# Summing the first mixer's conditioning vectors on VectorE instead of TensorE in the prologue of a two-layer block

## The chip, the cores and the metric

The kernel runs on one core of one Trainium2 chip. A core has TensorE (PE in the profile; its weight loads are shown as PEld), VectorE (DVE), ScalarE (ACT), GpSimd (POOL) and SyncE (SP), which issues most of the DMAs. Each engine works through its own instruction stream in order, and engines wait for one another by semaphores. The metric is the device time of one execution in microseconds, as the median of several runs. The profile is one separate execution.

## The reference, cut to what matters

A block of two layers works on 512 tokens of 1024 channels, in fp32. Each layer has a mixer (a gated linear recurrence in layer 0, dilated attention in layer 1) and a feed-forward part. Six conditioning vectors per layer scale, shift and gate what goes in and out:

```python
cond = jax.nn.silu(c)                                     # c is 1 x 1024
mod = (cond @ ada_w[layer] + ada_b[layer])[:, None, :]    # ada_w[layer] is 1024 x 6144
sh1, sc1, g1, sh2, sc2, g2 = jnp.split(mod, 6, axis=-1)
u = rms_norm(h, norm_g[layer, 0]) * (1.0 + sc1) + sh1
y = hgrn2_mixer(u, ...)                                   # begins with u @ w_in, 1024 x 4096
```

The change touches `sh1` and `sc1` of layer 0, that is, two matrix-vector products of a 1024 x 1024 block of `ada_w[0]` with `cond`, and the fp32 copy of `u` that they give.

## The kernel before

Products of fp32 accuracy are made of three TensorE passes over operands split in a rounded high part (`hi`, type fp32r) and the rest (`lo`): high by high, low by high, high by low. ScalarE makes the high part, and VectorE subtracts it from the fp32 original to make the low part.

The prologue (everything up to `pre.close()`) normalises and transposes the input to `xnT` (channels on the partitions, eight channel blocks of 128, 512 tokens each), finds `sh1` and `sc1`, makes `u` and its parts `uh` and `ul`, and computes the value projection `v_tok` of the first mixer. It goes through the eight channel blocks `e` in turn. For each block it needs

- `first[e]`, 1 MB: the columns of `ada_w[0]` that give `sh1` and `sc1` of this block, laid out as 8 row blocks `kt` of 128 rows on the partitions, each with 2 x 128 columns. Three buffers hold it; `load(e)` fetches it and the block's 128 rows of the value weights (512 KB).
- `group_steps(e)` (line 1523): eight TensorE matmuls of 256 columns in the code (16 in the profile, each with its weight load) that sum the eight row blocks, weighted with `cond`, into one PSUM bank with the partial sums spread over the partitions; ScalarE copies them to `facc` (line 1526).
- `sum_steps(e)` (line 1531): two TensorE matmuls of one column each (four in the profile), which sum `facc` over the partitions.
- `col_steps(e)` (lines 1536 and 1538): three VectorE instructions on 128x1, which add the bias and make the two columns of `cols`.
- `u_hi(e)` (line 1543): ScalarE makes `uh` of the block as `xnT * scale + shift`.
- `u_lo(e, ...)` (lines 1549 and 1550): VectorE makes the fp32 `u` in the same way, and then `ul = u - uh`.
- `w_hi(e)` and `w_lo(e)` (lines 1559 and 1562): ScalarE and VectorE split the value weights of the block.
- `v_pass(e, which, hf, t)` (line 1568): one TensorE pass of 512 columns. `which` 0 needs `uh` and the high weights, 1 needs `ul`, 2 needs the low weights. In the loop each `which` has seven passes, one for each tile in `tiles` (four token tiles by two column halves, less one); the eighth tile has no free PSUM bank and is made up at the end, in 18 passes after block 6 and 6 after block 7.

The prologue stands under `manual_schedule` for TensorE, VectorE, ScalarE and GpSimd, so these four run their instructions in the order in which the code is written. Only the order on SyncE's DMA queue is left to the compiler. In the loop over `e` from 1 to 7, the code for block `e` contains the conditioning of block `e + 1`: `group_steps(e + 1)` stands behind the `which` 0 passes, `sum_steps`, `col_steps`, `u_hi` and `u_lo` of block `e + 1` stand between the `which` 1 and the `which` 2 passes. Block 4's weights are split at the end of turn 2 and not at the start of turn 3, and turns 2 and 3 also hold a few small operations on the lower bounds (`lower_a` on ScalarE, `lower_b`, four VectorE instructions). After `u_hi(7)` the weights of the next stage are fetched by `st.fill()`, split in pieces (lines 135 and 136), and the main stage begins with TensorE matmuls on line 1856. The rest of the kernel, with an order by a planner whose costs are constants in the code, is not touched.

## Time and profile before

| what | value |
|---|---|
| median of 3 runs | 1436.22 us (1434.48 to 1436.47) |
| the profiled execution's own time | 1430.78 us |
| its span | 1429.0 us |
| TensorE busy | 1402.2 us, 98% of the span |
| VectorE busy | 1151.8 us, 81% |
| ScalarE busy | 823.5 us, 58% |
| start of the last value pass of the prologue | 73.05 us |
| start of the first matmul of the main stage | 73.27 us |

Times in a timeline are counted from the start of the span. A row of the timeline gives start, duration, engine, line, operation, what is written and read, and, in brackets, how long the engine sat idle before it and which instruction ended that. Successive instructions of one engine can overlap in these records, so what matters for a sequence is the distance from start to start. In a view by groups a row gives the number of instructions, their busy time in us and the mean of one in ns.

### The profile page before, as it was taken

The page shows a single profiled execution, that of the slowest core. Times are in us where ns is not written, and L with a number is a line of the kernel's source. Part 1 is how long each engine was busy: PE and PEld are TensorE (multiplying, and loading weights), DVE is VectorE, ACT ScalarE, POOL GpSimd, SP SyncE. Part 2 cuts the span into 40 slices and gives each one's busy share as a digit, 9 for nine tenths or more (in the row PEclk, how much of TensorE's full clock was granted, in tenths as well). Part 3 has the DMA queues.
Part 4 walks back from the last instruction along what each step waited for, and adds up shares of the span by engine and source line. Part 5 has one row for each costly group of instructions (what it writes and reads, how often), then busy time and mean ns, then how long its engine had stood idle before and what let it go on. Part 6 is the DMA issues. An engine that isn't in the chain of part 4 may idle for free. (4 is left out here: it accounts for less than half of the span.)

```text
span 1429.0 us, 25206 instructions
## 1 busy us (share of the span) xinstructions
PE 1402.2 (98%) x9785; PEld 1300.5 (91%) x9785; DVE 1151.8 (81%) x1838; ACT 823.5 (58%) x1539; POOL 208.5 (15%) x179
## 2 busy tenths in 40 slices
PE   8999999999999999999999999999999999999998
PEld 6788999899999988888989999999988899999887
DVE  4599889587888799778888977888776978888994
ACT  4443434465555643376648878477885555656651
POOL 1023112130111113140001010001012211110020
PEclk9999999999999999999999999999999999999999
DMA  9665655132344378423254452444362334334451
GB/s 309 180 207 191 206 178 177 60 110 73 114 119 119 118 248 290 138 95 122 93 152 126 111 154 66 122 138 130 99 200 87 104 104 119 111 104 163 155 177 59
DMA packets 213896, 201.09 MB, mean 141 GB/s; under 512 B 8920, under 2 KB 170640, under 8 KB 213520
## 3 DMA queue, kind: packets, MB, share of 16 engines
q1 hardware_dynamic: 210800, 192.71, 43.2%
q10 hardware_dynamic: 1952, 6.65, 1.3%
q8 instruction: 77, 1.26, 0.4%
q0 software_dynamic: 1024, 0.12, 0.2%
q14 instruction: 43, 0.35, 0.1%
HBM read 192.30 MB, written 5.30 MB: 138 GB/s over the span
## 5 line engine op out<-in xcount | busy, mean ns | idle before, releaser
L1856 PE MATMUL ps_mm<-apart,hiq 128*128 128x256 f32 (+1 forms) x608 | 137.4, 320 | 2.0 <-ACT xs L2348 1.2
L1856 PE MATMUL ps_mm<-uh,hiq 128*128 128x256 f32 (+1 forms) x416 | 134.5, 323 | 0.0
L1856 PE MATMUL ps_mm<-uh,loq 128*128 128x256 f32 (+1 forms) x416 | 131.1, 315 | 0.2 <-DVE loq L2281 0.2
L1856 PE MATMUL ps_mm<-ul,hiq 128*128 128x256 f32 (+1 forms) x416 | 131.0, 315 | 0.0
L1856 PEld LDWEIGHTS ps_mm<-apart,hiq 128*128 128x128 f32 x608 | 99.9, 191 | 8.3 <-ACT xs L2348 1.8
L967 DVE TENSOR_TENSOR loq<-raw,hiq 128x1024 fp32r<-128x1024 f32 x72 | 85.0, 1221 | 20.1 <-ACT hiq L963 20.1
L976 PE MATMUL ps_mm<-th,hiq 128*128 128x256 f32 x360 | 99.0, 275 | 0.0
L976 PE MATMUL ps_mm<-tl,hiq 128*128 128x256 f32 x360 | 99.0, 275 | 0.0
L976 PE MATMUL ps_mm<-th,loq 128*128 128x256 f32 x360 | 99.0, 275 | 0.0
L1856 PE MATMUL ps_mm<-apart,loq 128*128 128x256 f32 (+1 forms) x304 | 95.4, 314 | 0.6 <-DVE loq L2370 0.6
L947 POOL TENSOR_TENSOR raw<-raw 128x512 f32<-128x512 f32 x36 | 47.9, 1331 | 320.0 <-DVE spare L943 165.2
L963 ACT CAST hiq<-raw 128x1024 fp32r<-128x1024 f32 x72 | 72.3, 1049 | 21.2 <-DVE raw L951 16.6
L1856 PEld LDWEIGHTS ps_mm<-uh,loq 128*128 128x128 f32 x416 | 79.4, 191 | 4.7 <-DVE loq L2281 0.4
L1856 PEld LDWEIGHTS ps_mm<-uh,hiq 128*128 128x128 f32 x416 | 79.4, 191 | 4.4 <-issue 0.2
L1856 PEld LDWEIGHTS ps_mm<-ul,hiq 128*128 128x128 f32 x416 | 79.4, 191 | 4.1 <-issue 0.5
L976 PEld LDWEIGHTS ps_mm<-th,hiq 128*128 128x128 f32 x360 | 69.1, 192 | 0.1
L976 PEld LDWEIGHTS ps_mm<-tl,hiq 128*128 128x128 f32 x360 | 69.1, 192 | 0.0
L976 PEld LDWEIGHTS ps_mm<-th,loq 128*128 128x128 f32 x360 | 69.1, 192 | 0.0
L1856 PEld LDWEIGHTS ps_mm<-apart,loq 128*128 128x128 f32 x304 | 58.0, 191 | 3.9 <-DVE loq L2370 1.0
L596 PE MATMUL ps_mm<-ul,hi 128*128 128x256 f32 (+1 forms) x176 | 55.3, 314 | 1.6 <-DVE ul L695 1.6
L595 PE MATMUL ps_mm<-uh,hi 128*128 128x256 f32 (+1 forms) x176 | 55.4, 315 | 0.0
L597 PE MATMUL ps_mm<-uh,lo 128*128 128x256 f32 (+1 forms) x176 | 55.2, 314 | 0.0
(547 smaller groups left out, 4840.7 us busy)
## 6 DMA issues: line engine op xcount, KB each, us to landing
raw<-in_ffn_w_in_dram SPq DMA_DIRECT2D x144, 256.0 KB, 4.0
raw<-in_ada_w_dram SPq DMA_DIRECT2D x30, 1024.0 KB, 6.1
raw<-in_attn_w_in_dram SPq DMA_DIRECT2D x64, 256.0 KB, 4.2
raw<-in_ffn_w_out_dram SPq DMA_DIRECT2D x13, 1024.0 KB, 5.5
raw<-in_attn_w_in_dram SPq DMA_DIRECT2D x12, 1024.0 KB, 5.2
raw<-in_hgrn_w_in_dram SPq DMA_DIRECT2D x11, 1024.0 KB, 5.3
rawx<-in_ffn_w_out_dram SPq DMA_DIRECT2D x9, 1024.0 KB, 6.1
third<-in_ada_w_dram SPq DMA_DIRECT2D x8, 1024.0 KB, 7.0
```

Of the source, the lines that this page charges most:

```text
L595: pe.matmul(ps, ah, bh, start=start, stop=False, skip_group_check=part)
L596: pe.matmul(ps, ah, bl, start=False, stop=False, skip_group_check=part)
L597: pe.matmul(ps, al, bh, start=False, stop=stop, skip_group_check=part)
L947: pool.tensor_add(r[:, 2], r[:, 2], r[:, 0])
L963: act.copy(hi, src)
L967: dve.tensor_sub(lo, src, hi.bitcast(F32))
L976: pe.matmul(LAID(ps), w[x][:, a], TAKE(us[kt][y]), start=begin and kt + m == 0, stop=kt == 3 and m == 2, skip_group_check=True)
L1856: pe.matmul(LAID(dst()), x, TAKE(y), start=begin and i == 0, stop=i == len(todo) - 1, skip_group_check=True)
```

## The change

For the channel blocks 2 to 7 the sum over the row blocks is made by VectorE: `group_on_dve(e)` is one `tensor_scalar` and seven `scalar_tensor_tensor` on 128x256, each of which reads the result of the one before. `sum_steps` is as before and now sums this accumulator (`dacc`, two buffers) over the partitions. Blocks 0 and 1 keep `group_steps`. The sum of block `e + 2` is written into turn `e`, behind `u_lo(e + 1)`; `sum_steps`, `col_steps`, `u_hi` and `u_lo` of block `e + 1` move ahead of the `which` 1 passes. For blocks 2 to 7 the fp32 copy `u` is made by ScalarE, behind `u_hi`, and VectorE keeps the subtraction. The load of block 4 moves ahead of the loop, and in the loop `load(e + 4)` stands in place of `load(e + 3)`.

```diff
@@ -1525,6 +1525,14 @@
             accs_of[e] = fresh(sp, [P, 2, P], "facc", 1)
             act.copy(accs_of[e], ps.rearrange("p (v n) -> p v n", v=2))
 
+        def group_on_dve(e):
+
+            a = accs_of[e] = fresh(sp, [P, 2, P], "dacc", 2)
+            both = lambda t: t.rearrange("p v n -> p (v n)")
+            dve.tensor_scalar(both(a), both(first[e][:, 0]), cond[:, 0:1], None, op0=OP.mult)
+            for kt in range(1, KT):
+                dve.scalar_tensor_tensor(both(a), both(first[e][:, kt]), cond[:, kt:kt + 1], both(a), op0=OP.mult, op1=OP.add)
+
         def sum_steps(e):
 
             for v in (1, 0):
@@ -1546,7 +1554,10 @@
             if e not in us:
                 us[e] = fresh(sp, [P, S], "u", 2)
             u = us[e][:, tok]
-            dve.tensor_scalar(u, xnT[:, e, tok], cols[:, 1, e:e + 1], cols[:, 0, e:e + 1], op0=OP.mult, op1=OP.add)
+            if e > 1:
+                act.activation(u, xnT[:, e, tok], AF.Identity, bias=cols[:, 0, e:e + 1], scale=cols[:, 1, e:e + 1])
+            else:
+                dve.tensor_scalar(u, xnT[:, e, tok], cols[:, 1, e:e + 1], cols[:, 0, e:e + 1], op0=OP.mult, op1=OP.add)
             sub.tensor_sub(ul[:, e, tok], u, uh[:, e, tok].bitcast(F32))
 
         def w_tiles(q):
@@ -1673,21 +1684,24 @@
             col_steps(1)
             u_hi(1)
             u_lo(1, dve)
+            load(4)
+            group_on_dve(2)
             for e in range(1, KT):
                 if e + 1 < KT and e != 3:
                     w_hi(e + 1)
                     w_lo(e + 1, dve)
-                for which in (0, 1):
-                    for i in tiles:
-                        v_pass(e, which, *i)
-                    if which == 0 and e + 1 < KT:
-                        group_steps(e + 1)
+                for i in tiles:
+                    v_pass(e, 0, *i)
                 if e + 1 < KT:
                     sum_steps(e + 1)
-                    load(e + 3)
                     col_steps(e + 1)
                     u_hi(e + 1)
                     u_lo(e + 1, dve)
+                    load(e + 4)
+                if e + 2 < KT:
+                    group_on_dve(e + 2)
+                for i in tiles:
+                    v_pass(e, 1, *i)
                 if e == 2:
                     w_hi(4)
                     w_lo(4, dve)
```

## The prediction

> **What bounds the kernel now.** I read the page's head first, then the first 75 us, where all edits lie: a table of busy times in stretches, then the timeline of one turn of the loop, engine by engine.

> ```profile
> span 1429.0 us, 25206 instructions
> PE 1402.2 (98%) x9785; PEld 1300.5 (91%) x9785; DVE 1151.8 (81%) x1838; ACT 823.5 (58%) x1539; POOL 208.5 (15%) x179
> 50.00:60.00 10.00, 10.00 (x71) 7.07 (x69) 5.43 (x11) 3.87 (x5) 0.00 (x0) 1.00 0.20 69
> ```

> TensorE is idle for at most 27 us of the span, so the end of the prologue moves the end of the kernel nearly one to one. In the loop TensorE is full, VectorE 54%, ScalarE 39%, and GpSimd has nothing. The TensorE timeline of one turn, and of the last conditioning sum and what follows it:

> ```profile
> 42.82 0.50 PE L1531 MATMUL ps_b<-ones,facc 128*128 128x1 f32 x4
> 46.47 1.07 PE L1523 MATMUL ps_b<-first,cond_tiles 128*32 128x256 f32 x16
> 47.47 0.70 PE L1568 MATMUL ps_a<-hi,ul 128*128 128x512 f32 x2
> 49.08 0.50 PE L1531 MATMUL ps_b<-ones,facc 128*128 128x1 f32 x4
> ...
> 61.60 0.50 PE L1531 MATMUL ps_b<-ones,facc 128*128 128x1 f32 x4
> 61.96 0.68 PE L1568 MATMUL ps_a<-late,uh 128*128 128x512 f32 x2
> 63.55 0.38 PE L1568 MATMUL ps_b<-hi,uh 128*128 128x512 f32 x1
> 73.27 0.38 PE L1856 MATMUL ps_mm<-uh,hi 128*128 128x512 f32 x1
> ```

> A turn takes 49.08 - 42.82 = 6.26 us, of which the sum over row blocks takes 1.00. That is what the change takes off TensorE: about 5.3 us a turn would be left if nothing else waited. VectorE and ScalarE in such a turn:

> ```profile
> 30.91 0.16 DVE L1536 TENSOR_TENSOR cols<-ps_b,adab 128x1 f32<-128x1 f32 x1 [2.79 <-PE ps_b L1531]
> 31.11 0.16 DVE L1538 SCALAR_TENSOR_TENSOR cols<-cols,smallB 128x1 f32<-128x1 f32 x1
> 31.18 0.15 DVE L1536 TENSOR_TENSOR cols<-ps_b,adab 128x1 f32<-128x1 f32 x1
> 31.44 0.55 DVE L1549 TENSOR_SCALAR u<-xnT,cols 128x512 f32<-128x512 f32 x1
> 32.22 0.69 DVE L1550 TENSOR_TENSOR ul<-u,uh 128x512 fp32r<-128x512 f32 x1 [0.23 <-ACT uh L1543]
> ...
> 31.37 0.81 ACT L1543 ACTIVATE uh<-xnT,cols 128x512 fp32r<-128x512 f32 x1 [2.12 <-DVE cols L1536]
> 32.09 1.03 ACT L1559 CAST hi<-raw 128x1024 fp32r<-128x1024 f32 x1
> ```

> VectorE's longest wait of the turn, 2.79 us, is for TensorE's sum. The reader is to see that VectorE has room as a share, but in the written order that room lies ahead of the column step, while everything the change adds lies in one loop: sum on TensorE, columns, `uh`, `u`, `ul`, next group on VectorE, next sum.

> **The change, part by part.** Six groups (blocks 2 to 7) leave TensorE, and with them six ScalarE copies `facc`. VectorE gets six chains of one `tensor_scalar` and seven `scalar_tensor_tensor` on 128x256, each reading the last one's result. No such chain is in the trace; the nearest is the same sum with 512 columns, in the next stage:

> ```profile
> 78.66 0.75 DVE L1803 SCALAR_TENSOR_TENSOR shared<-raw,cond,shared 128x512 f32<-128x512 f32 x1
> 79.32 1.22 DVE L1906 TENSOR_TENSOR loq<-raw,hiq 128x1024 fp32r<-128x1024 f32 x1
> 80.46 0.74 DVE L1803 SCALAR_TENSOR_TENSOR shared<-raw,cond,shared 128x512 f32<-128x512 f32 x1
> 81.24 3.11 DVE L1803 SCALAR_TENSOR_TENSOR shared<-third,cond,shared 128x512 f32<-128x512 f32 x4
> ...
> 73.44 0.49 DVE L1801 TENSOR_SCALAR shared<-raw,cond 128x512 f32<-128x512 f32 x1 [0.57 <-DMA raw<-in_ada_w_dram]
> 73.96 0.75 DVE L1803 SCALAR_TENSOR_TENSOR shared<-raw,cond,shared 128x512 f32<-128x512 f32 x1
> ...
> 10.96 0.75 DVE L1501 TENSOR_SCALAR late<-h,rr 128x1024 f32<-128x1024 f32 x1 [0.67 <-POOL rr L1498]
> ...
> L1550 DVE TENSOR_TENSOR ul<-u,uh 128x512 fp32r<-128x512 f32 x7 | 4.8, 693 | 2.0 <-ACT uh L1543 2.0
> L1550 DVE TENSOR_TENSOR ul<-u,uh 128x256 fp32r<-128x256 f32 x1 | 0.4, 425 | 0.1
> L1803 DVE SCALAR_TENSOR_TENSOR shared<-raw,cond,shared 128x512 f32<-128x512 f32 x10 | 8.2, 822 | 0.0
> ```

> Four in a chain take 3.11 us; with 0.75 for the last, the start-to-start distance is (3.11 - 0.75) / 3 = 0.787. An independent successor starts after 79.32 - 78.66 = 0.66. Going from 512 to 256 columns saves 0.693 - 0.425 = 0.268 on a two-input operation (the pair on line 1550): so 0.52 from link to link and 0.39 from the last link to whatever follows. The first operation, from 0.75 at 1024 and 0.49 at 512, comes to about 0.36, and with the 0.03 that 73.44, 0.49 and 73.96 leave, to 0.39. The chain holds VectorE for **g = 0.39 + 6 x 0.52 + 0.39 = 3.9 us** (an estimate from these rows). Below, if links did not wait for one another: 0.39 + 7 x 0.39 = 3.1. Above, by the mean 0.82 of line 1803 in place of 0.75: 3.9 + 7 x 0.07 = 4.4. I take 3.9, since the chain of four has the same form and operands.

> *The copy `u`* moves from VectorE (0.55) to ScalarE. It stands behind `uh`, which another ScalarE operation follows after 32.09 - 31.37 = 0.72, and lasts 0.81 like `uh`. The subtraction now waits for it, where it waited for `uh`: 0.72 later. In the written order nothing can use VectorE in that time, because the next group stands behind the subtraction. So this edit costs 0.72 a block on the loop.

> [...]

> What else is in the loop: from VectorE's subtraction to its successor, the four small operations of `lower_b`, the first subtraction of the loop, and the way of a finished sum through TensorE:

> ```profile
> 44.74 0.69 DVE L1550 TENSOR_TENSOR ul<-u,uh 128x512 fp32r<-128x512 f32 x1 [0.30 <-ACT uh L1543]
> 45.35 0.20 DVE L1578 RECIPROCAL lbt<-lbt 128x8 f32<-128x8 f32 x1
> 46.06 1.22 DVE L1562 TENSOR_TENSOR lo<-raw,hi 128x1024 fp32r<-128x1024 f32 x1
> ...
> 25.96 0.69 DVE L1550 TENSOR_TENSOR ul<-u,uh 128x512 fp32r<-128x512 f32 x1 [0.30 <-ACT uh L1543]
> ...
> 23.44 0.37 ACT L1526 COPY facc<-ps_b 128x256 f32<-128x256 f32 x1 [2.62 <-PE ps_b L1523]
> 24.05 0.50 PE L1531 MATMUL ps_b<-ones,facc 128*128 128x1 f32 x4
> 24.66 0.16 DVE L1536 TENSOR_TENSOR cols<-ps_b,adab 128x1 f32<-128x1 f32 x1 [2.18 <-PE ps_b L1531]
> ```

> Behind the chain VectorE has `w_lo` of the next block: 80.46 - 79.32 = 1.14 to its successor. In that time the sum goes through TensorE: `facc` is ready at 23.81, the matmul starts 0.24 later, the column step 0.85 later. From the end of the chain's last link (0.10 after `w_lo` starts) that makes 0.95, under 1.14. So `w_lo`, not TensorE, sets when the columns begin, and TensorE waits for VectorE.

> The loop from one column step to the next: 0.46 to `uh` (31.37 - 30.91), 0.72 to `u`, 0.81 for it, 0.04 to the subtraction (32.22 after the end of `uh` at 32.18), 0.61 to the group (45.35 - 44.74), 3.9 for the group, 1.14 for `w_lo`: **7.68 us, where a turn takes 6.26 now.** TensorE has some 5.1 to 5.3 of work in it and idles the rest, about 2.5 us.

> Now the whole. The subtraction of block 1 starts at 25.96 as before; the group of block 2 at 26.57, `w_lo(2)` at 30.47, its column step at 31.61. Five more loops of 7.68, and the 0.71 of `lower_b` (46.06 - 45.35), which then lies between a group and a `w_lo`, put the column step of block 7 at 70.72. `w_lo(7)` starts 1.14 before, the chain ends 0.10 after that, the sum starts 0.24 later at 69.92, and the next pass 0.36 after it (61.96 - 61.60) at 70.28, against 61.96 now. Behind it now stand not only the seven `which` 2 passes but also the `which` 1 passes of block 6, which were ahead of it: seven more, 63.55 - 61.96 = 1.59. The rest up to line 1856 (11.3 us from 61.96 to 73.27) is the same. **The main stage starts 8.32 + 1.59 = 9.9 us later**, and each 0.1 us of g moves that by 0.6.

> What is hidden: the loads. Block 5's buffer comes free with the group of block 2, at 30.6, and is wanted about 20 us later; with it go the DMAs on SyncE's queue behind it.

> ```profile
> DMA to landing us min/median/max: 4.3/6.9/9.0
> ```

> With 9.0 us at most, no group waits for data; without that cover each us late would count in full.

> **The clock.** TensorE's new idle time may cost clock. Early in the prologue it stalled, and the granted clock fell:

> ```profile
> 14.74 1.06 PE L1506 MATMUL ps_mm<-ident,late 128*128 128x128 f32 x8 [1.53 <-DVE cols L1536]
> ...
> 16.00:18.00 2.00, 1.51 (x5) 0.82 (x6) 2.00 (x3) 0.88 (x2) 0.85 (x1) 0.53 1.12 345
> 18.00:20.00 2.00, 2.00 (x10) 1.94 (x10) 1.83 (x4) 1.30 (x3) 0.00 (x0) 0.62 1.15 312
> ```

> After an idle time of 1.53 us the clock was 0.53 and 0.62 over two stretches of 2 us: 2 x 0.47 + 2 x 0.38 = 1.7 us of TensorE's time lost. Within a turn the 2.5 us of idle time takes that up; after the last sum nothing does. I take half, 0.9, as one case does not tell whether each such stall brings it; ends 0 and 1.7.

> [...]

> **Sum:** 9.9 + 0.9 = 10.8 us. The profiled execution took 1430.78, so it would take 1441.6; the median of the runs lies 5.4 higher, at 1436.22, and the forecast is **1447.0 us**. Ends: g of 3.1 and no clock loss, 9.9 - 4.8 = 5.1; g of 4.4 and 1.7, 9.9 + 3.0 + 1.7 = 14.6. That is 1441.3 to 1450.8; the runs before spread over 2 us.

> **Rivals.** A difference under 0.2% (2.9 us) can't be told from none.

> *The fixed part of a VectorE operation hides.* Short operations follow each other by 31.18 - 31.11 = 0.07. If each link cost only its 0.268 of elements and 0.07, g would be 8 x 0.34 = 2.7, the loss 9.9 - 7.2 = 2.7, the time 1438.9: no difference. Against it: in the chain of four the same sum leaves 0.787 - 0.536 = 0.25. [...] Chance 0.08.

> [...] Chance 0.06.

> *TensorE at half clock becomes the bound.* If each stall brought the low clock for the whole turn, its 21 passes and the sum would take about twice 5.1, 10.2 against 7.68: 5 x 2.5 = 12.5 more, 1459.5. Against it: without idle time the clock came back within 4 us. Chance 0.06.

> **How the numbers follow.** The forecast as reckoned, within its ends, has 0.78, the three rivals 0.08, 0.06 and 0.06; 0.02 is left for a loss between 2.9 and 5.1. Slower: 0.78 + 0.06 + 0.02 = 0.86; same 0.08; faster 0.06. The range takes the forecast's ends and the runs' spread: 1440 to 1452.

> **What would show it.** Right: the column step of block 7 near 70.7 and line 1856 from about 83 on; links of 128x256 some 0.52 apart; VectorE's subtraction waiting for ScalarE's `u`, not `uh`; six waits of TensorE's sum for `dacc`, about 2.5 us each; no wait for `first`. Wrong: TensorE without gaps in the loop, turns under 6.26 us, or a wait for a transfer there.

## The result

The changed kernel takes 1442.55 us (median of 6 runs, 1440.89 to 1447.96), the kernel before in the same comparison 1434.85 (6 runs, 1432.38 to 1436.47). The ratio is 1.0061, with a 95% interval of 1.0041 to 1.0082: slower by 6 to 12 us, 8.8 in the middle. A second comparison gave 1440.16 against 1431.93, ratio 1.006 (1.0045 to 1.0075). The forecast of 1447.0 was right in sign and about 2 to 3 us high in the difference (10.8). Medians and ratios here and below leave out one run of a later kernel, which took 2431.61 us at a granted clock of 0.555.

### The profile after

The head of the page of the changed kernel:

```profile
span 1439.7 us, 25039 instructions
PE 1399.5 (97%) x9689; PEld 1300.6 (90%) x9689; DVE 1169.5 (81%) x1880; ACT 824.9 (57%) x1539; POOL 205.3 (14%) x179
```

TensorE does less (1399.5 us against 1402.2), and the span is 10.7 us longer. The same views of the loop as before, from the timeline of the changed kernel: one turn on VectorE, then ScalarE's two operations, then TensorE.

```profile
38.50 0.15 DVE L1544 TENSOR_TENSOR cols<-ps_b,adab 128x1 f32<-128x1 f32 x1
40.50 0.69 DVE L1561 TENSOR_TENSOR ul<-u,uh 128x512 fp32r<-128x512 f32 x1 [1.59 <-ACT u L1558]
41.11 0.35 DVE L1532 TENSOR_SCALAR dacc<-first,cond 128x256 f32<-128x256 f32 x1
41.49 3.61 DVE L1534 SCALAR_TENSOR_TENSOR dacc<-first,cond,dacc 128x256 f32<-128x256 f32 x7
45.02 1.22 DVE L1573 TENSOR_TENSOR lo<-raw,hi 128x1024 fp32r<-128x1024 f32 x1
46.15 0.15 DVE L1544 TENSOR_TENSOR cols<-ps_b,adab 128x1 f32<-128x1 f32 x1
...
38.95 0.81 ACT L1551 ACTIVATE uh<-xnT,cols 128x512 fp32r<-128x512 f32 x1 [5.20 <-DVE cols L1544]
39.66 0.80 ACT L1558 ACTIVATE u<-xnT,cols 128x512 f32<-128x512 f32 x1
...
42.37 0.38 PE L1579 MATMUL ps_b<-hi,uh 128*128 128x512 f32 x1
45.15 0.61 PE L1539 MATMUL ps_b<-ones,dacc 128*128 128x1 f32 x4 [2.41 <-DVE dacc L1534]
```

From column step to column step: 46.15 - 38.50 = 7.65 us, where it was 6.26. Two waits now close the loop. VectorE sits 1.59 us before its subtraction until ScalarE has made `u`, with the next chain queued behind; and TensorE sits 2.41 us before the sum until the chain is done. VectorE's old wait for TensorE's sum (2.79) is gone: `w_lo` fills it. The waits of the loop in total, the end of the prologue on TensorE, and VectorE's subtraction of block 1:

```profile
PEld ps_b L1539 <- DVE dacc L1534: 14.7, 6, 3.5
PE ps_b L1539 <- DVE dacc L1534: 12.3, 6, 3.1
DVE ul L1561 <- ACT u L1558: 9.5, 6, 1.6
...
68.84 0.61 PE L1539 MATMUL ps_b<-ones,dacc 128*128 128x1 f32 x4 [0.72 <-DVE dacc L1534]
69.31 0.68 PE L1579 MATMUL ps_a<-late,ul 128*128 128x512 f32 x2
72.42 0.38 PE L1579 MATMUL ps_b<-hi,uh 128*128 128x512 f32 x1
82.13 0.38 PE L1870 MATMUL ps_mm<-uh,hi 128*128 128x512 f32 x1
...
25.18 0.69 DVE L1561 TENSOR_TENSOR ul<-u,uh 128x512 fp32r<-128x512 f32 x1 [0.30 <-ACT uh L1551]
```

The main stage starts at 82.13 (line 1870 is the old 1856), 8.86 us later than before, though the loop was entered 0.78 us earlier: VectorE's subtraction of block 1 starts at 25.18 and not at 25.96. So the measure from here on is the **distance** from that subtraction to the first matmul of the main stage: 47.31 us before, 56.95 after, **+9.64**. What follows the prologue (span less the start of the main stage) is 1355.8 before and 1357.6 after; the order of instructions there is the same in both kernels.

### The profile page after: what moved, and what is told of

It is laid out like the page before. It is cut to its first block, busy times and chain, and to the rows that moved or that the text cites. A ratio compares the mean times of both kernels' runs of the same rounds, so it can differ in the third digit from the quotient of the medians.

```text
span 1439.7 us, 25039 instructions
## 1 busy us (share of the span) xinstructions
PE 1399.5 (97%) x9689; PEld 1300.6 (90%) x9689; DVE 1169.5 (81%) x1880; ACT 824.9 (57%) x1539; POOL 205.3 (14%) x179
## 3 DMA queue, kind: packets, MB, share of 16 engines
q0 software_dynamic: 1024, 0.12, 0.2%
## 5 line engine op out<-in xcount | busy, mean ns | idle before, releaser
L595 PE MATMUL ps_mm<-uh,hi 128*128 128x256 f32 (+1 forms) x176 | 55.4, 315 | 0.0
```

What stands on the lines that cost most here:

```text
L595: pe.matmul(ps, ah, bh, start=start, stop=False, skip_group_check=part)
```

## The experiments

Ten other kernels were run, and the changed one and the one before once more. The turn is the usual distance between two sums on TensorE in the loop.

| kernel | turn, us | distance, us | after the prologue, us | median, us (runs) |
|---|---|---|---|---|
| before | 6.26 | 47.31 | 1355.8 | 1434.85 (6) |
| before, again | 6.26 | 47.30 | 1357.8 | 1434.05 (12) |
| changed | 7.66 | 56.95 | 1357.6 | 1442.55 (6) |
| changed, again | 7.65 | 58.62 | 1353.4 | 1440.16 (5) |
| changed, `u` on VectorE | 6.95 | 54.34 | 1357.1 | 1439.61 (1) |
| before, `u` on ScalarE | 6.26 | 48.00 | 1356.4 | 1432.18 (1) |
| changed, group ahead of subtraction | 5.98 | 48.44 | 1356.0 | 1433.65 (1) |
| changed, `which` 1 passes ahead of the sum | 7.66 | 55.45 | 1358.3 | 1440.47 (1) |
| changed, half the chain left out | 5.57 | 44.42 | 1356.4 | 1428.11 (1) |
| changed, waits filled with matmuls | 7.65 | 56.95 | 1355.7 | 1440.76 (6) |
| shared sum, half behind the sum | 6.22 | 47.42 | 1359.4 | 1434.31 (12) |
| shared sum, half ahead of pass 1 | 5.77 | 46.31 | 1361.5 | 1432.31 (12) |
| shared sum, half behind pass 1 | 6.53 | 48.31 | 1363.4 | 1437.48 (10) |
| the same, subtraction ahead of the chain | 5.76 | 44.36 | 1360.3 | 1433.04 (12) |

The single times of one kernel scatter by several us (1428.89 to 1440.03 for the kernel before in one comparison), so the mechanism is read from turn and distance.

### `u` back on VectorE

```diff
-            if e > 1:
+            if e > KT:
                 act.activation(u, xnT[:, e, tok], AF.Identity, bias=..., scale=...)
```

> The changed kernel with the fp32 copy u back on VectorE for all blocks; all else as changed. The measure is the distance from the start of VectorE's subtraction of block 1 (25.18 in the changed kernel, 25.96 in the one before) to the first matmul of the main stage (82.13 and 73.27): 56.95 us after the change, 47.31 before it. Theory (a closed loop sum, columns, uh, u, ul, next group): the subtraction waits only for uh again, so a turn falls by 0.71, from 7.66 to 6.95, and the distance by six times that, to 52.7, although VectorE gets 0.55 us of work more in each turn. Rival (VectorE's amount of work is what counts): the turn grows by up to 0.55, to 8.2, and the distance to about 60.

```profile
48.23 0.69 DVE L1561 TENSOR_TENSOR ul<-u,uh 128x512 fp32r<-128x512 f32 x1 [0.30 <-ACT uh L1551]
```

The turn is 6.95, exactly as the theory had it, with 0.55 us more of work on VectorE: the wait counted, not the work. The distance is 54.34 and not 52.7. The expectation took six times the saving, but block 1's `u` is on VectorE in both kernels, so only five turns gain: 56.95 - 5 x 0.71 = 53.4. The remaining 0.9 is one turn of 7.8, in which the granted clock was low for 6.8 us (0.57 between 30 and 38); TensorE had no wait left ahead of that turn's sum that could take it up.

### Only `u` on ScalarE, in the kernel before

```diff
+            if e > 1:
+                act.activation(u, xnT[:, e, tok], AF.Identity, bias=..., scale=...)
+            else:
+                dve.tensor_scalar(u, xnT[:, e, tok], ...)
```

> The kernel before, with the fp32 copy u of blocks 2 to 7 made by ScalarE and nothing else changed. Theory: without a group behind it on VectorE the later subtraction is hidden by TensorE's passes, the turn stays at 6.26 and the distance at 47.3. Rival (the move costs 0.7 a block wherever it stands): 51.6.

The turn is 6.26, the distance 48.00 and not 47.3: hidden in all turns but two, of 6.85 and 6.37 us. In the first of these, the turn with `lower_a`, ScalarE's two table loads, 1.28 us each, already held up `facc` (they start at 39.40 and 40.91 in the kernel before, the copy at 42.31, the sum at 42.82), and `u` in front of them pushes it past the time when TensorE wants it:

```profile
43.04 0.20 ACT L1578 ACTIVATE warm<-ones 128x1 f32<-128x1 f32 x1
43.15 0.35 ACT L1526 COPY facc<-ps_b 128x256 f32<-128x256 f32 x1
...
43.55 0.61 PE L1531 MATMUL ps_b<-ones,facc 128*128 128x1 f32 x4 [0.44 <-ACT facc L1526]
```

So the same edit costs 0.7 in all where no chain stands behind it, and 0.7 a turn where one does.

### The group ahead of the subtraction

```diff
                     u_hi(e + 1)
-                    u_lo(e + 1, dve)
+                    u_lo(e + 1, dve, with_sub=False)
                     load(e + 4)
                 if e + 2 < KT:
                     group_on_dve(e + 2)
+                if e + 1 < KT:
+                    u_sub(e + 1)
```

> The changed kernel with the group of block e + 2 ahead of the subtraction of block e + 1 on VectorE, so that the group runs while ScalarE makes uh and u; the same instructions, in another order. Theory: the wait of 1.59 us leaves the loop, which becomes VectorE's work alone: 0.35 for the columns, 3.91 for the group, 0.61 for the subtraction, 1.14 for the low weights, together 6.0 us a turn; the distance falls by 5 x 1.65 and 0.6 more at the last sum, to 48.1, so still no gain on the kernel before (47.3). Rival (the order doesn't matter, VectorE or TensorE is simply slower): 7.66 a turn, 57.

```profile
45.44 0.15 DVE L1544 TENSOR_TENSOR cols<-ps_b,adab 128x1 f32<-128x1 f32 x1
45.77 0.35 DVE L1532 TENSOR_SCALAR dacc<-first,cond 128x256 f32<-128x256 f32 x1
46.15 3.61 DVE L1534 SCALAR_TENSOR_TENSOR dacc<-first,cond,dacc 128x256 f32<-128x256 f32 x7
49.68 0.68 DVE L1565 TENSOR_TENSOR ul<-u,uh 128x512 fp32r<-128x512 f32 x1
```

The same instructions in another order: the turn falls from 7.66 to 5.98 (6.0 expected) and the distance to 48.44 (48.1), 8.5 us less. VectorE has no gap left in these rows; the 1.59 us before `ul` is gone. The distance is still 1.1 us over that of the kernel before: up to the first of the six sums it takes 0.31 us more, and behind the last one 1.77 more (the seven passes moved there are most of it), while the turns between bring only 0.95.

### The `which` 1 passes ahead of the sum

```diff
                 for i in tiles:
                     v_pass(e, 0, *i)
+                for i in tiles:
+                    v_pass(e, 1, *i)
                 if e + 1 < KT:
                     sum_steps(e + 1)
...
                     group_on_dve(e + 2)
-                for i in tiles:
-                    v_pass(e, 1, *i)
```

> The changed kernel with the seven which-1 passes of each block back ahead of the sum of the next block on TensorE. Theory: TensorE has 2.4 us to spare in a turn, so the turn stays at 7.66, and only the last block gains, 1.5 us (seven passes less behind the last sum): distance 55.4. Rival (the order on TensorE holds up the loop): a turn under 7.4 or over 7.9.

```profile
68.66 0.61 PE L1539 MATMUL ps_b<-ones,dacc 128*128 128x1 f32 x4 [2.06 <-DVE dacc L1534]
70.72 0.38 PE L1579 MATMUL ps_b<-hi,uh 128*128 128x512 f32 x1
```

The turn stays at 7.66, the distance is 55.45 (55.4 expected). From the last sum to the make-up passes it is 70.72 - 68.66 = 2.06 us, against 72.42 - 68.84 = 3.58 in the changed kernel: 1.5 of the loss is the order on TensorE.

### Half the chain

```diff
-            for kt in range(1, KT):
+            for kt in range(1, 4):
                 dve.scalar_tensor_tensor(both(a), both(first[e][:, kt]), cond[:, kt:kt + 1], both(a), op0=OP.mult, op1=OP.add)
```

> The changed kernel with only row blocks 0 to 3 in VectorE's chain; row blocks 4 to 7 are left out of both vectors for channel blocks 2 to 7, so the kernel computes less. Theory: four links less take 4 x 0.52 = 2.08 off the turn, 7.66 to 5.58, and 6 x 2.08 = 12.5 off the distance, 56.95 to 44.5. Rival (a fixed cost of the chain, or a wait for its data, dominates): the turn falls by less than 1.5. Rival (TensorE becomes the bound): the turn stops at TensorE's own 5.3 or above it with waits for uh.

```profile
36.69 0.69 DVE L1561 TENSOR_TENSOR ul<-u,uh 128x512 fp32r<-128x512 f32 x1 [1.59 <-ACT u L1558]
37.68 1.52 DVE L1534 SCALAR_TENSOR_TENSOR dacc<-first,cond,dacc 128x256 f32<-128x256 f32 x3
42.26 0.69 DVE L1561 TENSOR_TENSOR ul<-u,uh 128x512 fp32r<-128x512 f32 x1 [1.58 <-ACT u L1558]
```

Turn 42.26 - 36.69 = 5.57 (5.58 expected), distance 44.42 (44.5): each link of 0.52 stands in full on the path, six times over.

### The changed kernel and the kernel before, again

Both unchanged.

> The changed kernel as it is, once more, for a second trace and more times. Theory: distance 57.0 and turn 7.66 within 0.1, as they are set by VectorE and ScalarE; what the first trace lost beyond the prologue (2.2 us between 780 and 1040 us) comes out another way, since the order of instructions there is the same in both kernels. Rival (the change costs those 2.2 us): the same 2.2 us again.

> The kernel before, unchanged, for a second trace. Theory: turn 6.26 and distance 47.3 within 0.1, as TensorE is never idle in the loop and nothing there can bring the low clock; the start of the loop and what follows the prologue differ by a few us from the first trace, as they do between the two traces of the changed kernel. Rival (the loop itself varies): a distance over 48.

The loops repeat: turns of 7.65 and 6.26, and 47.30 for the distance of the kernel before. The second trace of the changed kernel has 58.62, 1.67 more than the first. The clock of TensorE right behind the last sum, in 2 us stretches, first of this second trace, then of the first one:

```profile
71.00:73.00 2.00, 2.00 (x7) 1.62 (x6) 0.48 (x4) 1.45 (x2) 0.00 (x0) 0.56 0.32 63
73.00:75.00 2.00, 2.00 (x7) 1.59 (x6) 0.69 (x1) 0.07 (x1) 0.00 (x0) 0.59 1.00 329
```

```profile
71.00:73.00 2.00, 2.00 (x11) 1.76 (x10) 0.69 (x1) 0.81 (x2) 0.00 (x0) 1.00 0.84 250
```

The granted clock was 0.56 and 0.59 over 4 us, 2 x (0.44 + 0.41) = 1.7 us lost behind the last sum, where nothing waits for VectorE any more; in the first trace it was 1.00 there. What follows the prologue took 1353.4 us in the second trace and 1357.6 in the first, and 1355.8 and 1357.8 in the two of the kernel before: the 2.2 us between 780 and 1040 us that the changed kernel's first trace lost are scatter, not a cost of the change.

### The waits filled with matmuls

```diff
                 if e + 1 < KT:
+                    for _ in range(10):
+                        pe.matmul(sums[:, 256:384], ones, ones, start=True, stop=True)
                     sum_steps(e + 1)
```

> The changed kernel with ten matmuls of ones by ones, 128 columns, into an unused part of the bank ahead of each of the six sums, so that TensorE isn't idle while it waits for VectorE's group. Theory: the distance stays at 57 (within 0.4), the granted clock has no stretch of 0.5 between 25 and 80 us, and as the low clock was hidden in the waits the time is that of the changed kernel within 1 us. Rival (the low clock after the stalls costs time, and makes the changed kernel's runs spread from 1441 to 1448): the median falls by 1.5 us or more and the runs come closer together.

The table of stretches of the filled kernel, then that of the changed one:

```profile
28.00:40.00 12.00, 11.19 (x73) 10.09 (x71) 9.88 (x23) 2.94 (x4) 0.00 (x0) 1.00 0.93 268
52.00:64.00 12.00, 10.91 (x73) 9.89 (x71) 9.80 (x25) 2.46 (x3) 0.00 (x0) 1.00 0.32 95
```

```profile
25.00:37.00 12.00, 8.71 (x32) 6.76 (x32) 9.69 (x22) 3.66 (x5) 0.00 (x0) 0.86 1.13 328
61.00:73.00 12.00, 11.09 (x46) 9.31 (x47) 8.04 (x19) 3.97 (x5) 0.00 (x0) 0.86 0.14 42
```

With TensorE busy the clock stays at 1.00 from 28 us on; the distance is 56.95, the same as in the first trace of the changed kernel, where the clock was low twice within the loop. So a low clock inside a turn of the changed kernel is hidden by the wait for VectorE, as the prediction had it. The median (1440.76, ratio 1.0056 with 1.0041 to 1.0071) is not to be told from the changed kernel's beside it (1440.16, 1.006): the clock is no main cause of the loss.

### Sharing the sum between the engines

Four versions try to keep what the change wanted: TensorE sums row blocks 0 to 3, VectorE adds 4 to 7 in a chain of four whose first link reads TensorE's half from PSUM; `u` is on VectorE, the `which` 1 passes stand ahead of the sum.

```diff
+        def half_on_pe(e):
+            ps = sums[:, 256:512]
+            for kt in range(4):
+                j = slice(32 * kt, 32 * kt + 32)
+                pe.matmul(ps[j], cond_tiles[:, kt], first[e][:, kt], start=True, stop=True, tile_position=(0, 32 * kt))
+        def rest_on_dve(e):
...
+            for kt in range(4, KT):
+                dve.scalar_tensor_tensor(both(a), both(first[e][:, kt]), cond[:, kt:kt + 1],
+                                         sums[:, 256:512] if kt == 4 else both(a), op0=OP.mult, op1=OP.add)
```

In the first version both stand behind `sum_steps(e + 1)`, the chain ahead of the subtraction.

> The sum of each of the blocks 2 to 7 shared: TensorE sums row blocks 0 to 3 (8 of the 16 matmuls), VectorE adds row blocks 4 to 7 to that in a chain of four, the first link of which reads PSUM; u on VectorE, the group ahead of the subtraction, the which-1 passes ahead of the sum. Theory: VectorE's turn is 0.35 + 0.5 + 1.95 + 0.61 + 1.14 = 4.6, under TensorE's, which is 6.26 less half of the group's 1.0, about 5.7: the loop is TensorE's again, the distance is 47.3 - 6 x 0.5 = 44.3, and the time 0.2% under the kernel before (ratio 0.998). Rival (the closed loop still binds): a turn of 6.3 or more, ratio 1.000 or above.

```profile
38.83 0.50 PE L1546 MATMUL ps_b<-ones,dacc 128*128 128x1 f32 x4
39.64 0.15 DVE L1551 TENSOR_TENSOR cols<-ps_b,adab 128x1 f32<-128x1 f32 x1
39.84 0.64 PE L1533 MATMUL ps_b<-first,cond_tiles 128*32 128x256 f32 x8 [0.51 <-DVE cols L1551]
45.05 0.50 PE L1546 MATMUL ps_b<-ones,dacc 128*128 128x1 f32 x4
```

A miss: the turn is 6.22 and not 5.7. TensorE's half writes to the bank from which VectorE reads the columns, and waits 0.51 us for that, behind the 0.5 us of the sum; ratio 1.0016 (1.0005 to 1.0027). The second version moves the half between the `which` 0 and 1 passes.

> As the shared sum before (TensorE row blocks 0 to 3, VectorE 4 to 7), but TensorE's half for block e + 2 stands between the which-0 and the which-1 passes (behind the which-1 passes in the first turn) and not right behind the sum, where it waited 0.51 us in each turn for VectorE to have read the columns from the same bank. Theory: that wait, and most of the 0.3 us of idle time at the two changes of operation, leave the loop, which is then TensorE's work: 21 passes of 0.216, 0.36 for the sum, about 0.6 for the half and 0.2 of gaps, 5.7 us a turn; the distance is 44.3 to 44.8, and the time 2.5 to 3 us under the kernel before (ratio 0.998). Rival (VectorE's loop still binds): a turn of 6.2 as in the shared sum before, ratio 1.000 or above.

```profile
34.91 0.64 PE L1533 MATMUL ps_b<-first,cond_tiles 128*32 128x256 f32 x8 [1.07 <-DMA first<-in_ada_w_dram]
...
42.86 0.50 PE L1546 MATMUL ps_b<-ones,dacc 128*128 128x1 f32 x4
48.63 0.50 PE L1546 MATMUL ps_b<-ones,dacc 128*128 128x1 f32 x4
```

The turn is 5.77 (5.7 expected), the distance 46.31 and not 44.3 to 44.8: one half waited 1.07 us for its data, and the first turn, with two halves, takes 6.5. Ratio 0.999 (0.9978 to 1.0002). The third puts the half behind the `which` 1 passes in every turn, to cover that wait.

> The shared sum with TensorE's half for block e + 2 behind the which-1 passes of block e, directly ahead of the sum, in every turn. In the run before, the half of block 4 waited 1.07 us for its data, which landed at 34.9; 1.5 us of passes more ahead of it cover that. Theory: turn 5.77 as before, no wait for data, the distance falls from 46.3 to 45.2, 2.1 us under the kernel before, ratio 0.9985. Rival (the data bound moves to another turn): a turn of 6.5 or more somewhere behind the first, distance 46 or above.

```profile
47.53 0.70 PE L1590 MATMUL ps_a<-hi,ul 128*128 128x512 f32 x2 [0.51 <-DVE ul L1572]
```

A miss: the wait for data went, but the chain, now held back to the end of the turn, stood ahead of the subtraction, and the passes waited for `ul` in each of five turns; turn 6.53, ratio 1.0019 (1.0007 to 1.0030). The fourth puts the subtraction ahead of the chain again.

> The shared sum with TensorE's half directly ahead of the sum, and VectorE's subtraction ahead of its chain again, as in the changed kernel. In the run before, the chain could start only behind the half, so the subtraction behind it was late and the which-1 passes waited for ul, 0.6 us in each of five turns. Theory: VectorE's turn (0.46 + 0.85 with the wait for uh + 0.61 + 1.95 + 1.14 = 5.0) fits into TensorE's, which is 5.8 with no wait for ul and none for data; the distance is 45.1, 2.2 us under the kernel before, and the ratio 0.9985. Rival (what follows the prologue takes back what is gained there, as it seemed to in the last two runs): distance 45.1 and yet a ratio of 1.000 or above.

```profile
42.30 0.61 PE L1546 MATMUL ps_b<-ones,dacc 128*128 128x1 f32 x4
48.05 0.61 PE L1546 MATMUL ps_b<-ones,dacc 128*128 128x1 f32 x4
```

Turn 5.76, no wait for `ul` or for data, distance 44.36 (45.1 expected): it is 2.95 us shorter than before. The time is 1433.04 against 1434.25, ratio 0.9993 (0.9980 to 1.0005), so no gain that can be told. In all four traces of the shared sum what follows the prologue took 1359.4 to 1363.4 us, and in the ten others 1353.4 to 1358.3. In these traces that takes the gain back; most of it goes between 700 and 1040 us, in the attention, where the second trace of the kernel before also lost 2.3 us against the first. Three of the four have a stretch of low clock between 740 and 780 us (0.73 and 0.84 over 4 us each from 740 on in the second version, 0.77 and 0.81 from 772 on in the fourth), which none of the ten others has; why TensorE waits longer there, and where the rest goes, was not settled.

## Why the prediction was right, and where it was off

- **The chain, g = 3.9.** 3.91 (from 41.11 to 45.02), links of 0.52. Halving the 512-column rows by the pair on line 1550 gave the right price for a form that the trace didn't have.
- **The loop, 7.68.** 7.65 to 7.66 from subtraction to subtraction in both traces of the changed kernel, and 8.38 to 8.39 in the turn with `lower_b`, made of the terms as reckoned. The experiments on order and length show that it is a loop of waits: 0.71 for `u`, 0.52 a link, 1.6 for the wait before `ul`, each with its own kernel.
- **The end of the prologue, +9.9.** +9.64. The column step of block 7 came at 69.84, 44.66 after the loop's start, where the prediction had 70.72 and 44.76. That the end of the kernel follows the end of the prologue nearly one to one held for the changed kernel within the scatter of what follows; for the last shared sum it did not, with 2.95 us less in the prologue and 1.2 less in the medians, which is not clear of noise.
- **The loads.** No group on VectorE waited for `first`, whose transfers landed 3.8 to 9.0 us after their issue.
- **The waits of the six sums.** 12.3 us and not some 15: in two turns the low clock stretched TensorE's work, so that it waited 0.72 and not 2.41. The longest, 3.13, is the turn with `lower_b`.
- **The clock, 0.9 taken between 0 and 1.7.** Both ends occurred: 0 in the first trace, 1.67 in the second. No trace shows the 0.9 itself, so that this term came out near the middle is luck. The early stall from which it was read behaved in the same way: in the second trace of the kernel before it lasted 1.94 us, and the clock from 16 to 20 us was 1.00. That a low clock is hidden inside a turn was shown by the filled waits: a distance of 56.95 us with the clock at 1.00 from 28 us on, and 56.95 with a mean of 0.86 over two stretches of 12 us.
- **`u` on ScalarE, 0.72 a block.** Over the six blocks that would be 4.3 us to gain with `u` on VectorE. Five turns gain 0.71, not six, which makes 3.55 us. The distance fell by 2.6, since in that trace 0.9 went to the low clock (0.57 between 30 and 38 us).
- **The sum of 10.8.** The medians differ by 7.7 and 8.2, the ratio gives 8.8 (5.9 to 11.8). The prologue accounts for 9.64, and 1.7 more when the clock falls behind the last sum. The difference to the medians is within what the rest of the program varies by from run to run, 4 us between the two traces of the changed kernel; which of it would remain with many more runs is open. Of the 4.45 us between 1447.0 and 1442.55, 1.37 comes from the median before, which fell from 1436.22 to 1434.85 with three more runs.
- **The rivals.** Links did not hide their fixed part (0.52 and not 0.34). The kernel did not come out faster, for which the chance given was 0.06: the turn is 7.65 to 7.66 us against 6.26, the ratio 1.0061. And TensorE at a low clock did not become the bound of the loop: with the clock at 1.00 the turn was 7.65 as well.

My reading of the early rows, that an idle time of 1.53 us brings a low clock, does not hold for the stalls of the loop, and no other border for the length of a stall fits them either. In the first trace of the changed kernel the clock fell behind stalls of 2.86 and 3.13 us and not behind two of 2.41; in the second it fell behind three of 2.40 to 2.41, and not behind one of 2.86. What told the stalls apart stands in the last section.

## What to carry to other kernels

Before work is moved to an engine that looks half idle, write down the closed loop that the work will stand in, in the written order of each engine, and add up its waits: here VectorE was busy for 2.9 of 6.26 us a turn, and yet the change made a loop of 7.66, with 1.59 us of waiting in front of an instruction that had the new work queued behind it. An operation moved to a third engine to relieve the second one can cost more than it saves if the second then waits for it in order: here it took 0.55 us of work off VectorE and added 0.71 to the turn. Reordering the same instructions took back 8.5 of the 9.6 us.

## What the runs showed of the hardware that was not expected

Apart from the last microseconds of the span, the stretches of low clock in all traces had one length, 3.41 us, or twice that, 6.83. They fell at different stalls in two runs of one kernel: at 30.9 and 61.7 us in the first trace of the changed kernel, at 40.5, 54.2 and 71.2 in the second. They cost time where TensorE had no wait that took them up: 0.9 us in the turn with `u` on VectorE, 1.67 behind the last sum in the second trace of the changed kernel.

```profile
26.85:30.26 3.41, 1.41 (x7) 0.90 (x5) 3.20 (x8) 0.52 (x1) 0.00 (x0) 1.00 1.00 352
30.27:33.68 3.41, 2.56 (x14) 2.32 (x15) 2.19 (x6) 1.12 (x2) 0.00 (x0) 1.00 1.17 317
50.75:54.16 3.41, 1.00 (x6) 0.54 (x4) 3.18 (x8) 0.00 (x0) 0.00 (x0) 1.00 0.14 33
54.17:57.57 3.40, 3.40 (x10) 2.91 (x11) 1.94 (x7) 1.32 (x2) 0.00 (x0) 0.50 0.15 34
```

The stall of 2.86 us is cut by a step's end, which leaves 2.00 us of idle time in one step, and the clock stays; the stall of 2.41 lies within one step, and the next step runs at 0.50. In the 14 traces, from 11 us after the start to a few us before the end, 20 steps at full clock had 2.01 us or more without a matmul (the one-column sums counted as none), and all 20 were followed by a low clock; of the some 5750 others only two were (1.97 and 1.66 us idle). So in these traces it counted how much of one step a stall filled, with the border at some 2.0 of 3.41 us, and not its length alone. Where the grid lies differs from run to run, which would make the loss behind the last sum, 0 or 1.67 us, a matter of chance. This is a count over traces; no experiment shifted a stall against the grid. The ends of matmuls are modelled, and with the sums counted as work the border is less sharp.

A TensorE matmul waited 0.51 us for a VectorE read of other columns of the same PSUM bank, and began 0.05 us after its end (39.79 and 39.84). In the first shared sum five of the halves waited so, 2.6 us together. The trace shows the wait and not its reason, and the matmul was not run without it.
